# A last sum put behind the reads of its place, last branch rows loaded into their tiles, first pair parts split later

## The chip, the cores and the metric

The kernel runs on one core of a Trainium2 chip. The metric is the device time of one execution in microseconds (us), the median over several runs. TensorE (PE) does the matrix products; VectorE (DVE), ScalarE (ACT) and GpSimd (POOL) prepare and evacuate them; SyncE (SP) issues most of the DMAs.

## The reference

One layer of a hybrid encoder works on two streams of D = 1024 features: 1024 tokens of a new stream and 64 of a running one, 1088 columns in all. Cut to what matters:

```python
xn   = rmsnorm(x);  proj = xn @ w_in      # z | xBC | dt | q | k | v | gates
y    = rmsnorm((ssd(conv(xBC), dt) + d * xs) * silu(z))
o    = rmsnorm(diff_attention(rope(rmsnorm(q)), rope(rmsnorm(k)), v))
mix  = sigmoid(g_ssm) * (y @ w_branch_ssm) + sigmoid(g_att) * (o @ w_branch_attn)
x    = x + mix @ w_out
ha, hb = split(rmsnorm(x) @ w_up)
x    = x + (silu(conv(ha)) * hb) @ w_down
dt   = softplus(dt_raw + bias)            # the chain of small steps on VectorE
```

All is float32. The results are the two streams, and the new keys, values, states and convolution tails.

## The kernel before

**Three products for one.** TensorE multiplies rounded operands (type fp32r), so each float32 operand is split in two: a *cast* on ScalarE makes the high part (hi), and a *subtraction* on VectorE makes the rest (lo = source - hi). A product is the three matmuls hi·hi, hi·lo and lo·hi for each 128 rows of the contraction. The function split (L413 the cast, L414 the subtraction) does this, in place where the source was loaded into the lo tile. The function weights (L154 to L156) does the same for a whole weight block.

**Pairs.** The input projection (in_pair, L644), the up projection (L1604) and the down projection (L1778) work on two row blocks and the two column halves at once and need seven products in place of eight, numbered p = 0 to 6. Each has a left operand (a quarter of the weight block or a sum of quarters) and a right operand: the parts b11, t2, b21, t3, t1, t4, b22, which are quarters of the activations or sums of them. Every product has two column halves s = 0, 1, each 12 matmuls of 128x272. The left sums are made on GpSimd by make_left: s1 = q21 + q22 (L557), s2 = s1 - q11 (L559), s3 = q11 - q21 in q21's place (L561), and the last one, q12 - s2, in q12's place (L575). q12 itself is the left of p = 2, so its place is first read by that split. lefts_at is the table that says at which step of a pair each left is loaded, summed and split.

**Pair stage's start.** The first two pairs run their products p = 0 and 2 together (the list both), while the right parts t3, t1 and t4 are loaded from p_sc into their lo tiles and split by split_part. The table LATER says behind which p of the first pair the remaining parts are split. steps() is the dt chain: about 15 small VectorE instructions of 128x288 (L700 to L717), taken one by one beside the next pair.

**Branches.** branch() runs three times: the attention branch, and the two halves of the ssm branch. For each turn of output rows m in TURNS (the first turn is m = 0 and 1 together) it goes over four column chunks of 272 and makes a product of 8 row tiles x 3 matmuls (L162 to L164). The first two branches load both halves of their operand, split already, straight into the tiles, four row tiles per DMA (L206). The last branch has y_sc in float32 and stages it: a row tile of 128x272 is loaded into one of a few buffers b_f (L211), cast (L212) and subtracted (L213), 32 times. The tiles b{half}{chunk} are those of the branch before, so each is written only when TensorE has read it for the last time. Beside each product of the last branch lie loads into side tiles b_g (L192), a tanh (L220), a sum and product (L230 to L233) and the split of the mixed result (L1441, L1442).

The order on each engine is that of a scheduler that takes the instructions in program order with priorities and the waits that the tiles' reuse needs; an engine works its own queue in that order, and a wait at its head holds all behind it.

Of the kernel before, what the change touches and what calls it, by code (L numbers as in the profile page):

```python
# [90 lines left out]
def hybrid_layer(ctx: ExitStack, tc: tile.TileContext, xT, xt, prm, cst, rope, wvd, win, wbs, wba, wout, wup, wdn,  # L91
# [91 lines left out]
    def k_rows(parts, c, s):  # L183
        return [[t[:, k % 4] for t in parts[f"b{k // 4 + 1}{c + 1}", s]] for k in range(KT)]

    def branch(stage, side, src, wts, gates, adds, out, step=1):

        def next_to(m, c, w):
            tiles = []
# [10 lines left out]
        for i, (c, w) in enumerate(CH):  # L200
            tiles = {(f"b{h + 1}{i // 2 + 1}", i % 2): units_of(f"b{h + 1}{i // 2 + 1}", i % 2) for h in range(2)}
            parts.append(k_rows(tiles, i // 2, i % 2))
            for k in range(0, KT, step):
                if stage is None:
                    for u, t in enumerate(tiles[f"b{k // 4 + 1}{i // 2 + 1}", i % 2]):
                        load(out=t.bitcast(F32),  # L206
                             in_=src[D * u + P * k : D * u + P * (k + step), c : c + w].rearrange("(k p) t -> p k t", p=P))
                else:
                    t = stage()[:, :w]
                    hi, lo = parts[-1][k]  # L210
                    load(out=t, in_=src[P * k : P * (k + 1), c : c + w])  # L211
                    S.copy(hi, t)  # L212
                    V.tensor_tensor(out=lo, in0=t, in1=hi, op=ALU.subtract)  # L213
        for ms in TURNS:
            wt = [weights(wts[m], KT, P) for m in ms]
            for (c, w), rows_of in zip(CH, parts):
# [23 lines left out]
    def run(gen):  # L240
        for _ in gen:
            pass
# [294 lines left out]
    def make_left(x, what, blocks):  # L537

        if what == "load":
            for step in ("q11", "q21", "q22", "q12", "s1", "s2", "s3"):  # L540
                make_left(x, step, blocks)
            return
        if what in quarter:
            i, j = int(what[1]) - 1, int(what[2]) - 1
            n = blocks[i].shape[1] // 2
            seen["left"] = load(out=quarter[what][:, :n], in_=blocks[i][:, n * j : n * (j + 1)])
            return
        if what in ("s1", "s2", "s3"):
# [6 lines left out]
            q11, s2, q12, q21, s1, q22, q12 = made[x]  # L555
            if what == "s1":
                G.tensor_tensor(out=s1, in0=q21, in1=q22, op=ALU.add)  # L557
# [336 lines left out]
    rest = [(p, s) for p in (1, 3, 4, 5, 6) for s in range(2)]  # L894
    pairs = [begun_in(0), begun_in(1)]
    left[1] = {0: [t[:, :512] for t in early[1]], 2: [t[:, 512:] for t in early[1]]}
    for i, x in enumerate(("t3", "t1")):
        for at in both:
            pairs[i].send(at)
        split_part(x, seen["copy"])  # L900
        with after("copy"):
            for _ in range((2, 1)[i]):
                more_left(0)
    quarter_places()
    for at, (p, s) in enumerate(rest):
        pairs[0].send((p, s))
# [330 lines left out]
    with (tc.tile_pool(name="sin", bufs=1) as sin, tc.tile_pool(name="sp", bufs=1) as sp,  # L1237
# [163 lines left out]
                    load(out=d, in_=t)  # L1401
            yield i

        def stage():
            return staged("b_f")

        def side():
            return bs.tile([P, 384], F32, name="b_g", tag="b_g", bufs=BG)

        def branch_tiles():  # L1410
            nonlocal bs
            cv_pool.release()
            bs = tc.alloc_tile_pool(name="bs", bufs=1, side="right")
            yield from branch(None, side, o_sc, wba, D, (), store(m_sc), 4)
            yield from branch(None, side, y_sc[: 2 * D], wbs[0], None, (), store(n_sc), 4)

        bs, late = None, chain(filler, branch_tiles())
        for i in scan():
# [543 lines left out]
```

## Time and profile before

| | |
|---|---|
| median of 3 runs | 2444.05 us (2440.38 to 2444.22) |
| the profiled execution | 2447.51 us, of it a span of 2445.7 us |
| granted TensorE clock, mean | 0.995 |
| busy: PE, DVE, ACT, POOL | 98%, 71%, 50%, 28% |
| DMA, mean over the span | 184 GB/s |

TensorE is busy nearly always. What the other engines do moves the time only where TensorE stands waiting, or where its granted clock is lowered. The wait view lists each such place, and the windows view counts the matmuls that started in a stretch: where nothing is waited for, 5 us hold 42 matmuls of the 272-column kind in its counting, those on an edge included.

### The profile page before, as it was taken

The page shows a single profiled execution, that of the slowest core. Times are in us where ns is not written, and L with a number is a line of the kernel's source. Part 1 is how long each engine was busy: PE and PEld are TensorE (multiplying, and loading weights), DVE is VectorE, ACT ScalarE, POOL GpSimd, SP SyncE. Part 2 cuts the span into 40 slices and gives each one's busy share as a digit, 9 for nine tenths or more (in the row PEclk, how much of TensorE's full clock was granted, in tenths as well). Part 3 has the DMA queues.
Part 4 walks back from the last instruction along what each step waited for, and adds up shares of the span by engine and source line. Part 5 has one row for each costly group of instructions (what it writes and reads, how often), then busy time and mean ns, then how long its engine had stood idle before and what let it go on. Part 6 is the DMA issues. An engine that isn't in the chain of part 4 may idle for free.

```text
span 2445.7 us, 49558 instructions
## 1 busy us (share of the span) xinstructions
PE 2394.6 (98%) x18744; PEld 2320.2 (95%) x18744; DVE 1729.0 (71%) x3114; ACT 1227.7 (50%) x2713; POOL 686.3 (28%) x757
## 2 busy tenths in 40 slices
PE   8999999999999999999999999999999999999998
PEld 8989989999999999998899999999999999999998
DVE  4687877758687786867678665656966756768865
ACT  7345464356565665657555553434533333353442
POOL 0032333201011010115333332003255554544344
PEclk9999999999999999999999999999999999999999
DMA  7855768664544444336797954765124424357975
GB/s 245 275 175 188 240 206 298 207 204 148 163 150 149 129 146 143 108 123 227 260 330 249 336 182 131 225 198 172 56 84 144 158 97 157 128 191 198 253 181 104
DMA packets 296625, 449.80 MB, mean 184 GB/s; under 512 B 37113, under 2 KB 192898, under 8 KB 296386
## 3 DMA queue, kind: packets, MB, share of 16 engines
q1 hardware_dynamic: 285346, 420.31, 52.2%
q0 software_dynamic: 11040, 26.34, 5.3%
q8 instruction: 147, 2.41, 0.4%
q14 instruction: 92, 0.75, 0.1%
HBM read 294.03 MB, written 152.50 MB: 183 GB/s over the span
## 4 chain that ended last, share of the span: by engine, by line
PE 47%; DVE 3%; DMA 3%; issue 1%; POOL 1%; ACT 1%; SPq 0%; POOLq 0%; DVEq 0%; ACTq 0%
PE mx L1604 13%; PE mx L1778 6%; PE mm L1604 5%; PE mm L162 3%; PE mm L164 3%; PE mm L163 3%; PE mx L164 3%; PE mx L162 3%; PE mx L163 3%; PE mm L1778 2%; PE ye L1296 1%; PE yi L1290 1%; PE stp L1302 1%; DMA b_f<-y_sc 1%; DMA bc<-a_sc 1%
## 5 line engine op out<-in xcount | busy, mean ns | idle before, releaser
L162 PE MATMUL mm<-b,w_hi 128*128 128x272 f32 x1576 | 465.9, 296 | 0.3
L164 PE MATMUL mm<-b,w_lo 128*128 128x272 f32 x1576 | 459.2, 292 | 0.0
L163 PE MATMUL mm<-b,w_hi 128*128 128x272 f32 x1576 | 457.5, 291 | 0.0
L162 PEld LDWEIGHTS mm<-b,w_hi 128*128 128x128 f32 x1576 | 296.8, 188 | 6.2 <-issue 4.4
L163 PEld LDWEIGHTS mm<-b,w_hi 128*128 128x128 f32 x1576 | 297.0, 189 | 2.9 <-issue 2.1
L164 PEld LDWEIGHTS mm<-b,w_lo 128*128 128x128 f32 x1576 | 296.5, 188 | 0.7 <-issue 0.2
L985 DVE SCALAR_TENSOR_TENSOR cc<-pre,par,cc 128x272 f32<-128x272 f32 (+1 forms) x288 | 140.2, 490 | 16.3 <-ACT cc L983 13.4
L1604 PE MATMUL mx<-m,w_hi 128*128 128x272 f32 x752 | 144.4, 289 | 1.6 <-ACT m L413 1.3
L1604 PE MATMUL mx<-n,wh 128*128 128x272 f32 x1080 | 143.8, 288 | 1.9 <-DVE u L1631 1.0
L162 PE MATMUL mx<-b,w_hi 128*128 128x272 f32 x472 | 138.4, 295 | 3.2 <-ACT b L212 1.7
L1604 PEld LDWEIGHTS mx<-n,wh 128*128 128x128 f32 x1080 | 138.3, 188 | 2.5 <-DVE u L1631 1.3
L156 DVE TENSOR_TENSOR w_lo<-w_f,w_hi 128x1024 fp32r<-128x1024 f32 (+1 forms) x82 | 102.7, 1254 | 53.7 <-ACT w_hi L155 47.4
L414 DVE TENSOR_TENSOR wh<-w_f,wh 128x512 fp32r<-128x512 f32 (+1 forms) x144 | 140.4, 975 | 0.0
L973 POOL COPY pre<-pre 128x3 f32<-128x3 f32 x72 | 22.7, 315 | 419.0 <-DVE cc L987 195.9
L1109 ACT ACTIVATE p_t<-sc,mx 128x512 f32<-128x512 f32 (+6 forms) x144 | 106.1, 739 | 64.9 <-DVE mx L1100 30.9
L557 POOL TENSOR_TENSOR ws<-w_f 128x512 f32<-128x512 f32 (+1 forms) x47 | 62.4, 1328 | 270.4 <-DVE u L683 134.4
L164 PE MATMUL mx<-b,w_lo 128*128 128x272 f32 x472 | 137.5, 292 | 0.3 <-DVE w_lo L156 0.3
L163 PE MATMUL mx<-b,w_hi 128*128 128x272 f32 x472 | 136.2, 289 | 0.4 <-DVE b L213 0.3
L155 ACT CAST w_hi<-w_f 128x1024 fp32r<-128x1024 f32 (+1 forms) x82 | 85.9, 1049 | 71.8 <-PE mm L163 49.0
L1604 PEld LDWEIGHTS mx<-m,w_hi 128*128 128x128 f32 x752 | 118.0, 188 | 2.0 <-ACT m L413 1.5
L1613 ACT ACTIVATE cc<-pre,par 128x544 f32<-128x544 f32 (+1 forms) x44 | 37.2, 846 | 146.8 <-DVE pre L1648 145.8
L1604 PE MATMUL mx<-m,w_lo 128*128 128x272 f32 x376 | 108.3, 288 | 0.0
(463 smaller groups left out, 7101.4 us busy)
## 6 DMA issues: line engine op xcount, KB each, us to landing
w_f<-in_win_dram SPq DMA_DIRECT2D x48, 512.0 KB, 4.0
w_f<-in_wup_dram SPq DMA_DIRECT2D x80, 256.0 KB, 2.6
bc<-a_sc SPq DMA_DIRECT2D x32, 512.0 KB, 5.5
w_f<-in_win_dram SPq DMA_DIRECT2D x60, 256.0 KB, 3.9
h_sc<-hb SPq DMA_DIRECT2D x44, 272.0 KB, 2.1
ht<-h_sc SPq DMA_DIRECT2D x22, 544.0 KB, 4.8
t_sc<-ht SPq DMA_DIRECT2D x22, 544.0 KB, 2.9
out_dram<-yq POOLq DMA_DIRECT2D x44, 272.0 KB, 6.0
```

The costliest lines, as they stand in the source:

```text
L155: S.copy(hi, w)
L156: V.tensor_tensor(out=lo, in0=w, in1=hi, op=ALU.subtract)
L162: PE.matmul(ps, a_hi, b_hi, start=i == 0, stop=False)
L163: PE.matmul(ps, a_hi, b_lo, start=False, stop=False)
L164: PE.matmul(ps, a_lo, b_hi, start=False, stop=i == n - 1)
L414: V.tensor_tensor(out=lo, in0=src, in1=hi, op=ALU.subtract)
L557: G.tensor_tensor(out=s1, in0=q21, in1=q22, op=ALU.add)
L985: V.scalar_tensor_tensor(cc[:, :m], pre[:, i : i + m], cw(i), cc[:, :m], ALU.mult, ALU.add)
L1109: act(p_t[:n, :nk], sc[c][:n, :nk], AF.Exp, bias=mx[:n, c : c + 1], accum_out=dst)
L1604: PE.matmul(ps, w[x][:, c], b[y][:, k], start=start and k == i == 0, stop=k == 3 and i == 2, skip_group_check=not start)
L1613: act(cc[:, :n], pre[h][:, :n], AF.Identity, bias=col(O_FB + f), scale=cw(0))
L1778: PE.matmul(ps, w[y][:, c], b[z][:, k], start=start and k == j == 0, stop=k == n - 1 and j == 2, skip_group_check=not start)
```

## The change

Three edits:

- The sum q12 - s2 becomes a step of its own, "s4", in make_left. It was issued at the split of p = 3; now lefts_at issues it at step 1 of its pair, behind the split of p = 5. In the pairs that token_major names (the last one of the up projection, and in the down projection the first and last of each four) it is issued at step 0, and the split of p = 6 moves from step 0 to step 2.
- The last branch loads y_sc straight into the lo tiles, four row tiles per DMA (8 loads of 128x4x272), and splits them there with split (8 casts and 8 subtractions of 128x1088). The buffers b_f are gone from it.
- In the pair stage's start the split of t3 comes behind the products p = 0 and 2 of both first pairs, and those of t1, t4 and b22 behind p = 1, 3 and 4 of the first pair's rest; before, t3 came between the two pairs, t1 behind them, t4 behind p = 1 and b22 behind p = 3.

```diff
@@ branch()
-    def branch(stage, side, src, wts, gates, adds, out, step=1):
+    def branch(halves, side, src, wts, gates, adds, out):
...
-            for k in range(0, KT, step):
-                if stage is None:
+            for k in (0, 4):
+                if halves:
                     for u, t in enumerate(tiles[f"b{k // 4 + 1}{i // 2 + 1}", i % 2]):
                         load(out=t.bitcast(F32),
...
                 else:
-                    t = stage()[:, :w]
-                    hi, lo = parts[-1][k]
-                    load(out=t, in_=src[P * k : P * (k + 1), c : c + w])
-                    S.copy(hi, t)
-                    V.tensor_tensor(out=lo, in0=t, in1=hi, op=ALU.subtract)
+                    hi, lo = tiles[f"b{k // 4 + 1}{i // 2 + 1}", i % 2]
+                    load(out=lo.bitcast(F32), in_=src[P * k : P * (k + 4), c : c + w].rearrange("(k p) t -> p k t", p=P))
+                    split(hi, lo, lo.bitcast(F32))
@@ make_left()
+            elif what == "s4":
+                G.tensor_tensor(out=q12, in0=q12, in1=s2, op=ALU.subtract)
...
-        if what == 3:
-            G.tensor_tensor(out=made[x][6], in0=made[x][6], in1=made[x][1], op=ALU.subtract)
@@ lefts_at()
-            todo += {0: [(x, 6)]}.get(at, []) if token_major(x) else {0: [(x, 4)], 1: [(x, 5)], 3: [(x, 6)]}.get(at, [])
+            todo += ({0: [(x, "s4")], 2: [(x, 6)]} if token_major(x) else {0: [(x, 4)], 1: [(x, 5), (x, "s4")], 3: [(x, 6)]}).get(at, [])
@@ input projection
-    LATER = {1: "t4", 3: "b22"}
+    LATER = {1: "t1", 3: "t4", 4: "b22"}
...
-    for i, x in enumerate(("t3", "t1")):
+    for i in range(2):
         for at in both:
             pairs[i].send(at)
-        split_part(x, seen["copy"])
         with after("copy"):
             for _ in range((2, 1)[i]):
                 more_left(0)
+    split_part("t3", seen["copy"])
@@ run
-    run(branch(stage, side, y_sc[2 * D :], wbs[1], 0, (n_sc, m_sc), mixed))
+    run(branch(False, side, y_sc[2 * D :], wbs[1], 0, (n_sc, m_sc), mixed))
```

Lines behind L200 are numbered 2 to 5 lower in the changed kernel.

The order on ScalarE at the start of the pair stage, before. t300 to t311 are the tiles of t3 (hi of column half 0, its lo; hi of half 1, its lo), t100 to t111 those of t1, t400 to t411 of t4; w_hi are left operands, u1, pre and ss are what the first two pairs evacuate.

```order
L413 CAST t300_1580<-t301_1581 128x1088
L413 CAST t310_1583<-t311_1584 128x1088
L413 CAST w_hi_1676<-ws1_1602 128x512
L413 CAST w_hi_1676<-w_f_1600 128x512
L667 ACTIVATE ss_1762<-pre_1657 128x544
L700 ACTIVATE st_1567<-dtt_96 128x288
L715 ACTIVATE st_1567<-par_81 128x32
L679 COPY u1_1615<-mx_1696 128x272
L689 COPY pre_1722<-mx_1682 128x272
L701 ACTIVATE st_1567<-st_1567 128x288
L689 COPY pre_1722<-mx_1696 128x272
L413 CAST t100_1586<-t101_1587 128x1088
```

And in the changed kernel:

```order
L665 ACTIVATE ss_1758<-pre_1657 128x544
L698 ACTIVATE st_1567<-dtt_96 128x288
L713 ACTIVATE st_1567<-par_81 128x32
L677 COPY u1_1615<-mx_1692 128x272
L699 ACTIVATE st_1567<-st_1567 128x288
L687 COPY pre_1718<-mx_1678 128x272
L687 COPY pre_1718<-mx_1692 128x272
L411 CAST w_hi_1734<-ws2_1603 128x512
L411 CAST t300_1580<-t301_1581 128x1088
L411 CAST t310_1583<-t311_1584 128x1088
L411 CAST t100_1586<-t101_1587 128x1088
L411 CAST t110_1589<-t111_1590 128x1088
```

The casts of t3 stood ahead of the left operand's; now they stand behind them, behind the first ScalarE steps of the dt chain and behind the two copies L687 of the second pair's p = 2, and the casts of t1 follow at once.

The order on VectorE at the same place, before. st, dt2 and dtt are the tiles of the dt chain, w_lo the left operand's lo.

```order
L414 TENSOR_TENSOR t301_1581<-t301_1581,t300_1580 128x1088
L414 TENSOR_TENSOR t311_1584<-t311_1584,t310_1583 128x1088
L414 TENSOR_TENSOR w_lo_1677<-ws1_1602,w_hi_1676 128x512
L414 TENSOR_TENSOR w_lo_1677<-w_f_1600,w_hi_1676 128x512
L681 TENSOR_TENSOR u2_1614<-mx_1748,u1_1613 128x272
L712 TENSOR_SCALAR dtt_96<-dtt_96 128x288
L702 TENSOR_SCALAR st_1567<-st_1567 128x288
L681 TENSOR_TENSOR u2_1614<-mm_1784,u1_1613 128x272
L703 RECIPROCAL st_1567<-st_1567 128x288
L704 TENSOR_TENSOR st_1567<-st_1567 128x288
L683 TENSOR_TENSOR u1_1613<-mx_1748,u1_1613 128x272
L414 TENSOR_TENSOR t101_1587<-t101_1587,t100_1586 128x1088
```

And in the changed kernel, from the reciprocal on:

```order
L702 TENSOR_TENSOR st_1567<-st_1567 128x288
L703 TENSOR_TENSOR dt2_1951<-st_1567 128x288
L705 TENSOR_SCALAR st_1567<-dt2_1951 128x288
L679 TENSOR_TENSOR u2_1614<-mm_1780,u1_1613 128x272
L707 SCALAR_TENSOR_TENSOR st_1567<-st_1567,dt2_1951 128x288
L412 TENSOR_TENSOR w_lo_1735<-ws2_1603,w_hi_1734 128x512
L707 SCALAR_TENSOR_TENSOR st_1567<-st_1567,dt2_1951 128x288
L412 TENSOR_TENSOR t301_1581<-t301_1581,t300_1580 128x1088
L707 SCALAR_TENSOR_TENSOR st_1567<-st_1567,dt2_1951 128x288
L412 TENSOR_TENSOR t311_1584<-t311_1584,t310_1583 128x1088
L707 SCALAR_TENSOR_TENSOR st_1567<-st_1567,dt2_1951 128x288
L412 TENSOR_TENSOR t101_1587<-t101_1587,t100_1586 128x1088
```

The first of t3's subtractions stood ahead of the left operand's and of the whole dt chain; now a large part of the dt chain (L702 to L707) stands ahead of it, and steps of L707 between it and the next ones.

The order on ScalarE where the last branch begins, before. w_hi_19453 and w_hi_19459 are the weights of its first turn, b_g copies evacuate the branch before.

```order
L212 CAST b2100_19310<-b_f_19340 128x272
L212 CAST b1110_19344<-b_f_19348 128x272
L155 CAST w_hi_19453<-w_f_19452 128x1024
L226 COPY b_g_19177<-mx_19178 128x272
L226 COPY b_g_19205<-mm_19206 128x272
L226 COPY b_g_19233<-mm_19234 128x272
L212 CAST b1110_19344<-b_f_19352 128x272
L212 CAST b1110_19344<-b_f_19356 128x272
```

And in the changed kernel, where these weights are called w_hi_19349 and w_hi_19355:

```order
L411 CAST b1100_19308<-b1101_19309 128x1088
L411 CAST b2100_19310<-b2101_19311 128x1088
L224 COPY b_g_19121<-mx_19122 128x272
L224 COPY b_g_19149<-mx_19150 128x272
L411 CAST b1110_19318<-b1111_19319 128x1088
L155 CAST w_hi_19349<-w_f_19348 128x1024
L224 COPY b_g_19177<-mx_19178 128x272
L224 COPY b_g_19205<-mm_19206 128x272
L224 COPY b_g_19233<-mm_19234 128x272
L411 CAST b2110_19320<-b2111_19321 128x1088
L411 CAST b1200_19328<-b1201_19329 128x1088
L155 CAST w_hi_19355<-w_f_19354 128x1024
```

The eight row tiles of chunk 0 and the first one of chunk 1 stood ahead of the first weights, each alone; now tiles of four row tiles are cast whole, and the cast of chunk 1's first tile (b1110) stands ahead of the first weights.

The order on SyncE's queue there, in the changed kernel, where before 29 of the 32 loads into b_f stood among the stores and side loads up to the end of the first turn. n_sc and y_sc are stores of the branch before and of the scan.

```order
L210 DMA b1101_19309<-y_sc_74 128x4x272
L210 DMA b2101_19311<-y_sc_74 128x4x272
L236 DMA n_sc_71<-b_g_19093 128x272
L1335 DMA y_sc_74<-y_18762 128x4x320
L210 DMA b1111_19319<-y_sc_74 128x4x272
L236 DMA n_sc_71<-b_g_19121 128x272
L210 DMA b2111_19321<-y_sc_74 128x4x272
L236 DMA n_sc_71<-b_g_19149 128x272
L210 DMA b1201_19329<-y_sc_74 128x4x272
L210 DMA b2201_19331<-y_sc_74 128x4x272
L236 DMA n_sc_71<-b_g_19177 128x272
L236 DMA n_sc_71<-b_g_19205 128x272
```

Six of the eight loads stand in these rows, the last two a row further on.

More of the change, by code (lines that the diff above doesn't have):

```diff
@@ L202, in branch @@
             parts.append(k_rows(tiles, i // 2, i % 2))
[L203 to L204 removed]
+            for k in (0, 4):
+                if halves:
                     for u, t in enumerate(tiles[f"b{k // 4 + 1}{i // 2 + 1}", i % 2]):
                         load(out=t.bitcast(F32),
[L207 removed]
+                             in_=src[D * u + P * k : D * u + P * (k + 4), c : c + w].rearrange("(k p) t -> p k t", p=P))
                 else:
[L209 to L213 removed]
+                    hi, lo = tiles[f"b{k // 4 + 1}{i // 2 + 1}", i % 2]
+                    load(out=lo.bitcast(F32), in_=src[P * k : P * (k + 4), c : c + w].rearrange("(k p) t -> p k t", p=P))
+                    split(hi, lo, lo.bitcast(F32))
         for ms in TURNS:
@@ L547, in make_left @@
             return
-        if what in ("s1", "s2", "s3"):
+        if what in ("s1", "s2", "s3", "s4"):
             if what == "s1":
@@ L554, in make_left @@
                 left.setdefault(x, {})
-            q11, s2, q12, q21, s1, q22, q12 = made[x]
+            q11, s2, q12, q21, s1, q22, q12 = made[x][:7]
             if what == "s1":
                 G.tensor_tensor(out=s1, in0=q21, in1=q22, op=ALU.add)
+            elif what == "s4":
+                G.tensor_tensor(out=q12, in0=q12, in1=s2, op=ALU.subtract)
             elif what == "s2":
@@ L1402, in scan @@
             yield i
-        def stage():
-            return staged("b_f")
         def side():
@@ L1413, in branch_tiles @@
             bs = tc.alloc_tile_pool(name="bs", bufs=1, side="right")
-            yield from branch(None, side, o_sc, wba, D, (), store(m_sc), 4)
-            yield from branch(None, side, y_sc[: 2 * D], wbs[0], None, (), store(n_sc), 4)
+            yield from branch(True, side, o_sc, wba, D, (), store(m_sc))
+            yield from branch(True, side, y_sc[: 2 * D], wbs[0], None, (), store(n_sc))
         bs, late = None, chain(filler, branch_tiles())
```

## The prediction

> **What bounds the kernel now.** I read the busy times first, then the list of all waits of TensorE (PE), and then the windows and timelines at the places that the change touches.
>
> ```profile
> PE 2394.6 (98%) x18744; PEld 2320.2 (95%) x18744; DVE 1729.0 (71%) x3114; ACT 1227.7 (50%) x2713; POOL 686.3 (28%) x757
> ```
>
> TensorE is busy for 2394.6 of the 2445.7 us span, so work on the other engines costs nothing unless TensorE stands for it. Three places of the change are in its list of waits: the pair stage's start (115 to 170 us), the start of the last branch (1500 to 1570) and the down projection's first pairs (2170 to 2300). At the first:
>
> ```profile
> PE mx L644 <- DVE t L414: 3.0, 2, 2.0
> PE mx L644 <- ACT u L679: 1.0, 1, 1.0
> PE mm L644 <- DVE w_lo L414: 0.8, 1, 0.8
> ```
>
> ```profile
> 130.00:135.00 5.00, 4.91 (x40) 4.69 (x39) 4.97 (x10) 3.76 (x9) 0.14 (x1) 1.00 0.87 282
> 135.00:140.00 5.00, 2.63 (x19) 2.19 (x18) 5.00 (x4) 3.15 (x5) 4.77 (x4) 1.00 0.77 233
> 140.00:145.00 5.00, 4.00 (x19) 3.68 (x19) 5.00 (x6) 3.30 (x5) 3.48 (x2) 0.56 0.52 178
> 145.00:150.00 5.00, 5.00 (x33) 5.00 (x33) 5.00 (x8) 2.10 (x4) 0.00 (x0) 0.76 0.14 56
> 150.00:155.00 5.00, 5.00 (x42) 5.00 (x41) 5.00 (x12) 1.94 (x3) 0.00 (x0) 1.00 0.51 164
> 160.00:165.00 5.00, 4.22 (x34) 4.01 (x33) 4.87 (x6) 0.00 (x0) 4.08 (x3) 1.00 0.14 52
> ```
>
> The columns of a window are its length, then busy us and count for PE, PE's weight loads, DVE, ACT and POOL, the granted clock, and the DMA share. An undisturbed stretch (150 to 155) holds 42 matmuls. A missing matmul is 5 / 42 = 0.12 us lost, so the rows from 130 to 150 lose (2 + 23 + 23 + 9) x 0.12 = 6.8 us, and that from 160 another 1.0. The wait is for the parts that VectorE subtracts, and VectorE is busy for 5.00 of 5 us from 135 on: here it is the bound. Two of the stretches also have a lower clock, 0.56 and 0.76, behind the wait of 2.0 us.
>
> At the last branch:
>
> ```profile
> PE mx L162 <- ACT b L212: 1.7, 1, 1.7
> PE mx L162 <- ACT w_hi L155: 0.9, 1, 0.9
> ```
>
> ```profile
> 1515.00:1520.00 5.00, 5.00 (x42) 5.00 (x41) 1.39 (x4) 2.71 (x6) 0.00 (x0) 1.00 0.43 134
> 1535.00:1540.00 5.00, 4.74 (x36) 4.36 (x35) 4.05 (x11) 2.23 (x7) 0.00 (x0) 1.00 0.81 232
> 1540.00:1545.00 5.00, 4.81 (x32) 4.07 (x32) 4.02 (x10) 3.03 (x8) 0.00 (x0) 1.00 0.86 264
> 1545.00:1550.00 5.00, 2.88 (x19) 2.21 (x17) 2.23 (x7) 2.33 (x6) 0.00 (x0) 1.00 0.91 273
> 1550.00:1555.00 5.00, 3.95 (x29) 3.73 (x30) 3.66 (x9) 2.90 (x6) 0.00 (x0) 1.00 0.92 303
> ```
>
> Here the clock stays at 1.00 and (6 + 10 + 23 + 13) x 0.12 = 6.2 us are lost. Who is late is read from the two lines of the staged rows:
>
> ```profile
> L212 ACT CAST b<-b_f x32: 415/420/439, 1507.5 to 1547.8; 128x272 fp32r<-128x272 f32 x32
> ...
>   DMA b_f<-y_sc: 11.6, 19
> ```
>
> ```profile
> L211 SPq DMA_DIRECT2D b_f<-y_sc x32: 319/358/502, 1362.6 to 1544.3; - x32
> ...
> DMA to landing us min/median/max: 2.0/2.7/6.6
> ```
>
> ScalarE has only 13.4 us of casts, but stood 19 times, 11.6 us in all, for a row tile to land: three buffers, a landing of 2.7 us each and a queue of side loads between them make the staging slow. It runs to 1548, while the first turn began at 1520.9. And because the cast of the next weights stands behind the last row tile on ScalarE,
>
> ```profile
> 1549.68 1.04 ACT L155 CAST w_hi<-w_f 128x1024 fp32r<-128x1024 f32 x1
> ```
>
> they come at 1549.68 to 1550.7, which is the wait of 0.9 for w_hi.
>
> **The last branch's loads.** Removed are 32 loads, 32 casts and 32 subtractions; added are 8 loads of 544 KB, 8 casts and 8 subtractions of 128x1088. In engine time little changes: a cast of that size takes 1.05 us (two in 2.10, at 132.69 below) against 4 x 0.42 = 1.7. The gain is in when the rows arrive. The loads have places of their own, each free when TensorE has read it for the last time in the branch before. In the trace of before SyncE issues row tiles here from about 1507 on,
>
> ```profile
> 1508.46 1.07 SPq L211 DMA_DIRECT2D b_f<-y_sc  x2
> ```
>
> and chunk 0 of the new order goes there. TensorE frees a chunk's place about 6 us behind the one before (48 matmuls of 0.12), and between the loads stand stores, each held by the ScalarE copy that it stores; so I estimate chunk 1 at 1513 to 1515.5, chunk 2 by 1518 and chunk 3 by 1522. No such load is in the trace at this place. The nearest rows, by size and source, are those of the branch before:
>
> ```profile
> L206 SPq DMA_DIRECT2D b<-y_sc x16: 370/773/1927, 1358.1 to 1391.0; - x16
> ...
> DMA to landing us min/median/max: 4.8/8.9/10.2
> ```
>
> With those of the attention branch, which the line counts too, their median landing is 8.9, in a crowded stretch; the small ones at this very place take 2.7. The window at 1515 has a DMA share of only 0.43, so I take 4.5, between the two. Chunk 3 is then ready by 1529 with cast and subtraction, and is wanted at 1539; even at 10.2 it would be in time. The casts of the first turn end 20 us earlier, and the next weights are cast as soon as they land. So of the 6.2 us lost I let 0.7 remain, for chunk 0 to 1: **5.5 us gained**. The cover is the landing of chunk 1's first tile: its cast stands on ScalarE ahead of the first weights' (w_hi_19349). With 4.5 us it lands at 1517.7, the weights are cast by 1520 and subtracted by 1521.3 where TensorE wants them at 1520.9. At 8.9 they come at 1525.5 instead, which takes 4.5 of the gain back. Ends: 6.2 gained, and 4 lost (second rival).
>
> **The pair stage's start.** Nothing is removed; splits move. On ScalarE:
>
> ```profile
> 126.10 2.13 ACT L413 CAST t<-t 128x1088 fp32r<-128x1088 f32 x2
> 128.10 0.64 ACT L413 CAST w_hi<-ws 128x512 fp32r<-128x512 f32 x1
> ...
> 132.41 0.39 ACT L689 COPY pre<-mx 128x272 f32<-128x272 f32 x1 [1.24 <-PE mx L644]
> 132.69 2.10 ACT L413 CAST t<-t 128x1088 fp32r<-128x1088 f32 x2
> ```
>
> Before, the casts of t3 were done at 128.2, and TensorE had its high part ready when it came to it. Now they stand behind the copy at 132.41, which itself waits for TensorE's last product with the old parts; a left operand's cast (0.64) lies between. So t3's first high part is ready at about 132.4 + 0.3 + 0.6 + 1.05 = 134.3, with TensorE through all it had by 132.3. It stands for some 2 to 3 us there, where before it had work until 136. Whether this sets the end is decided by VectorE:
>
> ```profile
> 127.26 2.50 DVE L414 TENSOR_TENSOR t<-t,t 128x1088 fp32r<-128x1088 f32 x2 [5.86 <-ACT t L413]
> ...
> 134.71 1.28 DVE L414 TENSOR_TENSOR t<-t,t 128x1088 fp32r<-128x1088 f32 x1
> ...
> 137.38 2.36 DVE L414 TENSOR_TENSOR t<-t,t 128x1088 fp32r<-128x1088 f32 x1
> ...
> 140.82 2.37 DVE L414 TENSOR_TENSOR t<-t,t 128x1088 fp32r<-128x1088 f32 x1
> ...
> 143.47 2.01 DVE L414 TENSOR_TENSOR t<-t,t 128x1088 fp32r<-128x1088 f32 x1
> 145.41 0.71 DVE L671 TENSOR_TENSOR ss<-ss,sq 128x544 f32<-128x544 f32 x1
> 146.04 0.44 DVE L709 SCALAR_TENSOR_TENSOR st<-st,dt 128x288 f32<-128x288 f32 x1
> ```
>
> Before, it was busy without a gap from t3's subtraction at 127.26 to the end of t4's at 145.48, which includes much of the dt chain. In the new order it does the same up to that point, and more: five steps L709 (0.37 each by the next start) and the sum L671 (0.63), less one copy of pre (0.35): 5 x 0.37 + 0.63 - 0.35 = 2.1 us. It starts 0.5 earlier, since the left operand's casts now come first, and stands about as long for the chain's first ScalarE steps; these two I set against each other. What I keep is that four subtractions take 2.0 to 2.4 instead of 1.28 and so does the work beside GpSimd's sums:
>
> ```profile
> 134.86 2.28 POOL L557 TENSOR_TENSOR ws<-w_f 128x512 f32<-128x512 f32 x1 [134.41 <-DVE u L683]
> ```
>
> GpSimd's four sums still run, at about the same time, and the loss of VectorE beside them (1.08 + 1.09 + 0.73 = 2.9 us on three subtractions) only falls on t3 and t1 instead of t1 and t4. So t4 is through at 147.6, **2.1 us later**. After it TensorE has 11 matmuls left of t4. Before, these lay in the slow clock:
>
> ```profile
> 355.60 4.61 PE L644 MATMUL mx<-b,wh 128*128 128x272 f32 x21 [2.49 <-ACT u L679]
> ```
>
> is another such stretch, 21 matmuls in 4.61 us, 0.22 each, against 0.12. The stand of 2 to 3 us now comes some 5 us earlier, and so does the slow stretch; it then lies where VectorE is the bound anyway, and the last 11 go at 0.12: 11 x 0.10 = 1.1 us back. Behind that, the five steps L709 are done already, so the dt chain no longer delays the w_lo that TensorE waited 0.8 us for at 164.8; I count half. Sum: 2.1 - 1.1 - 0.4 = +0.6, and with some slow clock left I take **+1.0**. Ends: -3 if VectorE's work no longer falls beside GpSimd's, +5 if slow clock comes on top.
>
> [...]
>
> **The last sum s4.** On GpSimd its order against the other sums is the same nearly everywhere, since no other GpSimd work stood between its old place and its new one; the wait for the readers of q12 holds nobody else there. I cost it at 0 in the up projection, and the DMA share of its loads too. In the token-major pairs the split of p = 6 goes two steps back on ScalarE and VectorE, and u of the down projection goes ahead of the w_lo. TensorE's waits there are
>
> ```profile
> PE mx L1778 <- DVE n L414: 2.9, 2, 2.7
> PE mm L1778 <- DVE w_lo L414: 1.2, 1, 1.2
> ```
>
> The 1.2 us could go, or grow by the 0.4 of that copy; the 2.7 us at 2290 are a subtraction far down VectorE's queue that the move hardly touches. I take 0, within 2 either way. That two GpSimd output DMAs swap with sums there is cost at 0, since the sums are made some steps ahead of their split.
>
> **The sum.** 2447.5 (the profiled execution, 3.5 above the median) - 5.5 + 1.0 + 0 = 2443.0; the same 4.5 us off the median of 2444.05 is **2439.5 us**. A measurement of this kernel can tell about 0.2%, 4.9 us, from no change: 2439.2 to 2448.9 count as the same.
>
> **The rivals.**
> First, the splits save more than counted: TensorE's slow clock does not come in the pair stage, and VectorE's subtractions run in 1.28 beside an idle GpSimd. For it: GpSimd's first sum waits for loads that the earlier left splits release. Against: they are only some 3 us earlier. Pair stage -3, branch -5.5: 2444.05 - 8.5 = 2435.5.
>
> Second, slower: the last branch's loads land late. Chunk 1's first tile holds ScalarE's queue and with it the first weights. For it: the rows of the branch before, up to 10.2 us; four loads of 544 KB beside stores of n_sc. At 10.2 the tile lands at 1523.4, the weights are through (1.05 + 1.05 + 1.3) at 1526.8, 5.9 us after TensorE wants them, and a stand that long brings the slow clock of the windows at 140 and 145, (23 + 9) x 0.12 = 3.8 us: 9.7 against 5.5 gained, so +4.2, with +1.0 from the pair stage +5.2: 2449.3. It turns to a loss at a landing of about 7 us, where the wait of 2.7 and a slow stretch are more than the gain. Against: the DMA share of 0.43.
>
> Third, no gain: the first turn is paced by its side loads as soon as the rows are not. Each product of the last branch wants three of them, SyncE issues them behind one another, and they are not changed. Then half the 6.2 us stays, 2444.05 - 3.1 + 1.0 = 2442. The same band holds a pair stage with the slow clock on top, +3.8: 2444.05 - 5.5 + 1.0 + 3.8 = 2443.4. Against: TensorE's waits name the row tile and the weights, never a side load.
>
> **How the numbers follow.** Forecast 0.45, its own range 2437 to 2442, half of it under 2439.2; first rival 0.19; second 0.20; third 0.16. Faster: 0.225 + 0.19 = 0.42. Same: 0.225 + 0.16 = 0.38. Slower: 0.20. The range takes the ends of the first and second rival, since neither alone is under one in ten: 2434.5 to 2449.5.
>
> **What would show it.** Right: in the windows 1535 to 1555 the counts are 42 again, no wait for a part of the last branch is left, and the third turn's w_hi is cast by about 1542. Between 130 and 155 the count is about 8 matmuls lower in sum, with TensorE standing near 133 and t4's last subtraction ending near 147.6; the slow windows come at 135 to 145. Wrong: a wait for w_hi or w_lo at 1521 (late landing), waits for side tiles in the first turn, clock under 1.00 behind 145, or a difference at a place that is not named here.

## The result

The changed kernel's median is 2437.84 us (20 runs, 2432.04 to 2442.49), that of before 2443.57 (20 runs, 2439.64 to 2447.65). The ratio is 0.9979, with a 95% interval of 0.9972 to 0.9987: 5.1 us less, between 3.2 and 6.8. The difference of the medians is 5.7. The profiled execution took 2441.61 us, against 2447.51 before.

The head of the page after has the span and the busy times:

```profile
span 2439.8 us, 49478 instructions
...
PE 2393.0 (98%) x18744; PEld 2320.5 (95%) x18744; DVE 1719.7 (70%) x3090; ACT 1222.0 (50%) x2689; POOL 690.9 (28%) x757
```

TensorE has the same work; the span is 5.9 us shorter. The windows at the last branch's start, after:

```profile
1520.00:1525.00 5.00, 4.01 (x31) 3.77 (x31) 4.63 (x5) 4.88 (x9) 0.00 (x0) 1.00 1.10 351
...
1535.00:1540.00 5.00, 5.00 (x42) 5.00 (x41) 3.52 (x9) 1.29 (x4) 0.00 (x0) 1.00 0.59 165
1540.00:1545.00 5.00, 5.00 (x42) 5.00 (x41) 2.65 (x8) 2.43 (x7) 0.00 (x0) 1.00 0.84 237
1545.00:1550.00 5.00, 5.00 (x40) 4.78 (x39) 4.79 (x10) 2.86 (x5) 0.00 (x0) 1.00 0.54 177
1550.00:1555.00 5.00, 5.00 (x42) 5.00 (x41) 2.47 (x7) 1.17 (x3) 0.00 (x0) 1.00 0.83 285
```

The counts are 42 from 1525 on, but for 40 at 1545. Where 6.2 us were lost there are now (11 + 2) x 0.12 = 1.6. The wait view of that place, and the line of the new loads:

```profile
PE mx L164 <- DVE w_lo L156: 1.0, 1, 1.0
```

```profile
L210 SPq DMA_DIRECT2D b<-y_sc x8: 359/378/512, 1507.0 to 1522.7; - x8
...
DMA to landing us min/median/max: 3.7/5.1/5.7
```

The row tiles are no longer waited for. What is left is one wait for the first weights' low part. The loads land in 5.1 us in the median, and the last one was issued at 1522.7, where the last staged row went at 1544.3.

The pair stage's start, windows and waits after:

```profile
130.00:135.00 5.00, 2.94 (x22) 2.50 (x20) 4.93 (x10) 2.93 (x5) 0.00 (x0) 1.00 1.05 390
135.00:140.00 5.00, 3.39 (x15) 2.86 (x15) 5.00 (x4) 5.00 (x6) 3.93 (x3) 0.67 0.82 264
140.00:145.00 5.00, 4.34 (x22) 4.03 (x23) 5.00 (x4) 3.18 (x5) 2.49 (x2) 0.65 0.15 52
145.00:150.00 5.00, 4.57 (x36) 4.34 (x35) 5.00 (x10) 0.00 (x0) 0.00 (x0) 1.00 0.00 0
150.00:155.00 5.00, 5.00 (x42) 5.00 (x41) 5.00 (x10) 2.46 (x4) 0.57 (x1) 1.00 0.14 56
160.00:165.00 5.00, 5.00 (x41) 4.89 (x40) 3.35 (x7) 1.18 (x2) 4.14 (x3) 1.00 0.30 108
```

```profile
PE mx L642 <- DVE st L707: 1.5, 1, 1.5
PE mm L642 <- DVE t L412: 1.5, 2, 0.8
PE mx L642 <- DVE t L412: 1.2, 2, 0.8
```

TensorE stands near 133, before the part t3 is split, and the lower clock (0.67 and 0.65) has moved forward, from the stretch of 140 to 150 to that of 135 to 145. The windows from 160 on are nearly full, where before 8 matmuls were missing. And the waits of the down projection's first pairs:

```profile
PE mx L1773 <- DVE n L412: 1.4, 1, 1.4
PE mm L1773 <- DVE u L1787: 0.9, 1, 0.9
PE mx L1773 <- DVE m L412: 0.7, 1, 0.7
PE mx L1773 <- DVE u L1778: 0.4, 1, 0.4
```

These are 3.4 us in four waits, where the two lines of before that the prediction shows were 4.1 us in three. That for n, at 2290 before, fell from 2.7 to 1.4. The clock behind it is the third number from the end of the windows. Before:

```profile
2290.00:2295.00 5.00, 4.51 (x23) 4.51 (x24) 5.00 (x8) 1.68 (x4) 0.97 (x2) 0.66 1.11 292
```

After:

```profile
2285.00:2290.00 5.00, 4.38 (x31) 3.99 (x32) 5.00 (x8) 2.52 (x4) 0.95 (x2) 1.00 1.11 292
```

The stretch of 0.66 has gone from this place, and 8 matmuls more stand in the 5 us. But the changed kernel has a lower clock behind the other three waits, near 2210, where before it had none:

```profile
2210.00:2215.00 5.00, 4.16 (x29) 3.51 (x27) 5.00 (x7) 3.80 (x7) 3.96 (x2) 1.00 0.08 30
```

After:

```profile
2210.00:2215.00 5.00, 3.87 (x18) 3.65 (x19) 5.00 (x9) 0.62 (x1) 0.19 (x1) 0.70 0.59 111
```

So in this profile the slow stretch has moved and not gone; what the down projection gains lies in the waits.

### The profile page after: what moved, and what is told of

Its sections match the earlier page's. It is cut to its first block, busy times and chain, and to the rows that moved or that the text cites. A ratio compares the mean times of both kernels' runs of the same rounds, so it can differ in the third digit from the quotient of the medians.

```text
span 2439.8 us, 49478 instructions
## 1 busy us (share of the span) xinstructions
PE 2393.0 (98%) x18744; PEld 2320.5 (95%) x18744; DVE 1719.7 (70%) x3090; ACT 1222.0 (50%) x2689; POOL 690.9 (28%) x757
## 4 chain that ended last, share of the span: by engine, by line
PE 47%; DVE 4%; DMA 2%; issue 2%; ACT 1%; POOL 0%; SPq 0%; POOLq 0%; DVEq 0%; ACTq 0%
PE mx L1599 13%; PE mx L1773 6%; PE mm L1599 5%; PE mm L162 3%; PE mm L164 3%; PE mm L163 3%; PE mx L162 3%; PE mx L164 3%; PE mx L163 3%; PE mm L1773 2%; PE yi L1288 1%; PE ye L1294 1%; PE stp L1300 1%; PE tr L1267 1%; DMA w_f<-in_wout_dram 1%
## 5 line engine op out<-in xcount | busy, mean ns | idle before, releaser
L1616 POOL TENSOR_TENSOR hb<-hb,cc 128x544 f32<-128x544 f32 (+2 forms) x63 | 67.0, 1078 | 132.6 <-DVE hb L1637 98.5
```

The source lines that it names most:

```text
L1616: (V if f + 1 == FT else G).tensor_tensor(out=hb[h][:, o : o + n], in0=hb[h][:, o : o + n], in1=cc[:, d : d + n], op=ALU.mult)
```

## The experiments

A single profile is moved by a few us of the attention and the scan, so beside the times each run is read by stage, from the starts of the same matmuls in each trace. The pair stage runs from TensorE's wait for u (L679) near 126 to that near 356; the last branch from its wait for grs near 1505, such as

```profile
1505.72 0.39 PE L162 MATMUL mx<-b,w_hi 128*128 128x272 f32 x1 [0.52 <-ACT grs L1327]
```

to the up projection's first wait, near 1732; the down projection from its first matmul on the part n (L1778) to the end of the span. A bar is where the trace has no such wait at the start. The last two columns are the median and the ratio to the kernel before, measured beside it.

| kernel | pair stage | last branch | down projection | median us | ratio, 95% |
|---|---|---|---|---|---|
| before | 229.9 | 231.5 | 250.7 | | |
| changed | 230.4 | 226.9 | 249.4 | 2437.84 | 0.9979 (0.9972 to 0.9987) |
| branch alone | - | 226.8 | 250.6 | 2437.57 | 0.9967 (0.9955 to 0.9980) |
| pair stage alone | 229.6 | 231.7 | 251.8 | 2445.23 | 1.0007 (0.9997 to 1.0016) |
| s4 alone | 230.0 | 231.9 | 248.2 | 2442.00 | 0.9988 (0.9979 to 0.9997) |
| in place, one row tile each | 230.5 | 227.9 | 249.8 | 2437.76 | 0.9968 (0.9956 to 0.9980) |
| staged, eight buffers | 230.0 | 228.0 | 250.9 | 2440.67 | 0.9973 (0.9963 to 0.9983) |
| changed, pair stage as before | 230.0 | 229.0 | 250.5 | 2439.07 | 0.9966 (0.9955 to 0.9977) |
| that, and weights first | - | 229.6 | 248.4 | 2439.88 | 0.9975 (0.9964 to 0.9986) |
| changed, t3 early | 228.8 | 228.2 | 248.4 | 2438.41 | 0.9974 (0.9965 to 0.9983) |

The medians of before beside them were 2444.91 (the four of the first group: branch, pair stage, s4, one row tile each) and 2446.07 (the other four).

Kernels that have the same order of instructions in a stage show how far one profile of it can be trusted. The last branch took 226.8 to 229.0 us in the four that load four row tiles at a time with the weights where they were, and 231.5 to 231.9 in the three that stage in three buffers. The down projection took 248.2 to 250.5 in the six with the new left splits, and 250.6 to 251.8 in the four with the old. The pair stage can be read more sharply up to the 283rd matmul behind its start, near 170: 44.2 to 44.5 us in the six kernels with the old splits, 44.9 in the three with the new ones (changed, pair stage alone, one row tile each), and 42.8 with t3 early.

**The three parts alone.** The branch's loading alone, in the kernel before:

```diff
-                    t = stage()[:, :w]
-                    hi, lo = parts[-1][k]
-                    load(out=t, in_=src[P * k : P * (k + 1), c : c + w])
...
+                    hi, lo = tiles[f"b{k // 4 + 1}{i // 2 + 1}", i % 2]
+                    load(out=lo.bitcast(F32), in_=src[P * k : P * (k + 4), c : c + w].rearrange("(k p) t -> p k t", p=P))
+                    split(hi, lo, lo.bitcast(F32))
```

> The kernel before with the last branch's loading alone changed (8 loads of four row tiles in place). Theory: nearly all of the gain is here. The time is 4.5 us under before (ratio 0.998), no wait for a row tile is left in the first turn, one wait of about 1 us for w_lo at 1522 stays, and what follows the branch stands 4.5 us earlier in the profile. Rival (the first turn is paced by its side loads, and the gain comes from the pairs): half of it at most, 0 to -2 us, with waits for side tiles in the first turn.

The ratio is 0.9967, 8.1 us less (4.9 to 11.0), and the last branch is 4.7 us shorter. TensorE's wait there is the one foretold:

```profile
PE mx L164 <- DVE w_lo L156: 1.0, 1, 1.0
```

The rival falls: no wait for a side tile. The time is lower than the stage accounts for: the interval ends at 4.9, just above it. In this profile the attention and the scan were 4.7 us shorter as well, which the last section takes up.

The pair stage's splits alone:

```diff
-    LATER = {1: "t4", 3: "b22"}
+    LATER = {1: "t1", 3: "t4", 4: "b22"}
...
+    split_part("t3", seen["copy"])
```

> The kernel before with the later splits of the pair stage's start alone. Theory: VectorE is the bound there and gets more to do ahead of t4's last subtraction, so that ends near 149 in place of 145.5; the slow clock moves to 135 to 145, where it is covered; the first matmul behind the stage stands 0.5 us later (within 1), the time is the same within 1.5 us. Rival (the split costs a stand of TensorE and a slow clock on top): +3 to +5 us. Second rival (the move is what gained): -2 us or more.

The ratio is 1.0007 (0.9997 to 1.0016), the stage 0.3 us shorter. Its windows:

```profile
130.00:135.00 5.00, 2.37 (x15) 1.73 (x13) 4.93 (x10) 3.88 (x6) 0.00 (x0) 1.00 1.05 386
135.00:140.00 5.00, 3.75 (x17) 3.42 (x18) 5.00 (x4) 4.91 (x7) 4.88 (x3) 0.60 0.67 214
140.00:145.00 5.00, 4.34 (x28) 4.02 (x27) 5.00 (x6) 2.42 (x4) 1.55 (x2) 0.72 0.15 52
```

The stand is at 130 to 135 (15 matmuls of 42) and the slow clock at 135 to 145, as in the changed kernel. Neither of the two rivals is borne out; a cost of up to 3.9 us is within the interval of the time. The length of the whole stage does not show one; up to the 283rd matmul the stage is 0.6 us longer than before.

The last sum's move alone:

```diff
+            elif what == "s4":
+                G.tensor_tensor(out=q12, in0=q12, in1=s2, op=ALU.subtract)
...
-        if what == 3:
-            G.tensor_tensor(out=made[x][6], in0=made[x][6], in1=made[x][1], op=ALU.subtract)
...
-            todo += {0: [(x, 6)]}.get(at, []) if token_major(x) else {0: [(x, 4)], 1: [(x, 5)], 3: [(x, 6)]}.get(at, [])
+            todo += ({0: [(x, "s4")], 2: [(x, 6)]} if token_major(x) else {0: [(x, 4)], 1: [(x, 5), (x, "s4")], 3: [(x, 6)]}).get(at, [])
```

> The kernel before with the last sum moved alone. Theory: the order on GpSimd hardly changes, so the time is the same within 1 us up to the down projection, and within 2 us at the end. Rival (the move relieves the token-major pairs): the waits at 2200 to 2220 and at 2290 fall by 2 us or more and the time by as much.

Here the rival came true. The ratio is 0.9988 (0.9979 to 0.9997), 2.9 us less, and the down projection is 2.5 us shorter. The wait for n fell from 2.7 to 0.7:

```profile
PE mx L1778 <- DVE n L414: 0.7, 1, 0.7
```

VectorE reached that subtraction earlier, and in part because it had waited less. ScalarE's casts of the parts ph, which come back from t_sc, show it. In the kernel before (the bracket is ScalarE's idle time, and what ended it):

```profile
2273.09 1.10 ACT L413 CAST ph<-ph 128x1088 fp32r<-128x1088 f32 x1 [2.48 <-DMA ph<-t_sc]
...
2277.04 1.10 ACT L413 CAST ph<-ph 128x1088 fp32r<-128x1088 f32 x1 [1.41 <-DMA ph<-t_sc]
```

With s4 and the split of p = 6 moved:

```profile
2266.37 1.10 ACT L413 CAST ph<-ph 128x1088 fp32r<-128x1088 f32 x1 [0.40 <-DMA ph<-t_sc]
...
2270.91 1.11 ACT L413 CAST ph<-ph 128x1088 fp32r<-128x1088 f32 x1
```

ScalarE stood 3.9 us for the two loads before, and 0.4 now; VectorE, whose subtractions of ph follow, had 1.4 us of waits for them and has none. In the four kernels with the old left splits (before, branch alone, pair stage alone, eight buffers) and the six with the new ones this divides without exception: 2.8 to 4.5 us in sum with the old, 0 to 0.6 with the new. So does the wait for n, 2.65 to 2.70 against 0.4 to 2.1.

The second of these ranges is wide, and the six kernels have the same order of instructions on every engine there. What tells them apart is the first of the subtractions of n. In the kernel before VectorE takes 2.38 us for it, beside GpSimd's third left sum (L561, from 2281.43 to 2283.18):

```profile
2281.95 2.38 DVE L414 TENSOR_TENSOR n<-n,n 128x1088 fp32r<-128x1088 f32 x1
```

With s4 alone it takes 1.28:

```profile
2276.21 1.28 DVE L414 TENSOR_TENSOR n<-n,n 128x1088 fp32r<-128x1088 f32 x1
```

Three of the six have 1.28 (s4 alone, weights first, t3 early), with a wait for n of 0.4 to 0.7 and a down projection of 248.2 to 248.4. The other three have 2.38 (changed, one row tile each, changed with the pair stage as before), with waits of 1.4 to 2.1 and 249.4 to 250.5. So the loads of ph are a part of the fall, and much of the rest goes with the time of that subtraction, 1.28 or 2.38 us, which differs between profiles of the same order.

Why the load of ph stands 2 us earlier is seen only in the order: on SyncE two loads of weights stand behind loads and stores of right parts that they stood ahead of, and on VectorE the sums that fill t_sc stand some rows further forward. Which of these does it was not tried. When the split of p = 6 is moved by itself, and the sum is left where it was, the order of the instructions is the same on every engine as with both. So the sum's own move does nothing that the order shows, and the gain is that of the later split of p = 6.

**What made the staging slow.** In place, with one row tile per load:

```diff
-                    load(out=lo.bitcast(F32), in_=src[P * k : P * (k + 4), c : c + w].rearrange("(k p) t -> p k t", p=P))
-                    split(hi, lo, lo.bitcast(F32))
+                    for r in range(4):
+                        load(out=lo[:, r].bitcast(F32), in_=src[P * (k + r) : P * (k + r + 1), c : c + w])
+                        split(hi[:, r], lo[:, r], lo[:, r].bitcast(F32))
```

> The changed kernel, with the last branch's rows loaded into place one row tile at a time: 32 loads of 128x272, 32 casts and 32 subtractions as before, but no staging buffers. If the place makes the gain (no load waits for a buffer to be emptied by VectorE), the time is within 1 us of the changed kernel and the first turn has no waits for rows. If the size of the loads makes it (few large transfers, few queue entries on SyncE and ScalarE), 3 us or more are lost again, with waits for row tiles in the first turn as before.

0.9968: the same as the large loads. In the first turn TensorE waits for no row tile. It waits for the first weights' low part (0.4), and once for the next weights:

```profile
PE mx L162 <- ACT w_hi L155: 1.7, 1, 1.7
...
PE mx L164 <- DVE w_lo L156: 0.4, 1, 0.4
```

And staged as before, but with eight buffers:

```diff
         def stage():
-            return staged("b_f")
+            staged_at[0] += 1
+            if staged_at[0] % 8 < 3:
+                return staged("b_f")
+            return bs.tile([P, 272], F32, name="b_f", tag="b_f", bufs=5)
...
-            return bs.tile([P, 384], F32, name="b_g", tag="b_g", bufs=BG)
+            return bs.tile([P, 272], F32, name="b_g", tag="b_g", bufs=BG)
```

> The kernel before, with staged row tiles in the last branch as they were, but eight buffers b_f instead of three (room for them comes from side tiles cut to the 272 columns that are used). Theory: what made the staging slow is that a load waits for a buffer to be read by ScalarE and VectorE. With eight the loads run ahead of the first turn, its waits for row tiles go, and 3 to 5 us are gained, nearly as much as by loading in place. Rival (32 small loads, casts and subtractions in queues with stores and side loads are slow by themselves): under 2 us gained, and waits for row tiles stay in the first turn.

0.9973, 6.6 us less, and the last branch 3.5 us shorter. The casts of the staged rows:

```profile
L212 ACT CAST b<-b_f x32: 412/420/440, 1505.3 to 1527.2; 128x272 fp32r<-128x272 f32 x32
...
  DMA b_f<-y_sc: 3.4, 4
```

They ended at 1527 instead of 1548, and ScalarE stood 3.4 us for rows in place of 11.6. So neither the size of the loads nor the number of casts made the staging slow, but the three buffers. How they did it stands in the order of SyncE's queue. With eight buffers every load is issued ahead of the first side load, the last at 1524.2 and the side load at 1524.6. With three, 17 of them stand among the side loads, from 1524.7 to 1544.3. Ahead of the loads SyncE waited 9.1 us from 1510 on with three buffers, 8.2 of it for VectorE, and 4.0 with eight. So a load could go only when its buffer had been read, and few buffers also put it far back in the queue.

**The rest.** The changed kernel with the pair stage as before:

```diff
-    LATER = {1: "t1", 3: "t4", 4: "b22"}
+    LATER = {1: "t4", 3: "b22"}
...
-    split_part("t3", seen["copy"])
```

> The changed kernel with the pair stage's splits where they were before. Theory: the later splits cost 0 to 1 us, so this is 0 to 1 us faster than the changed kernel and about 7 us (ratio 0.997) under before: 4.7 from the last branch, 2 from the down projection. Rival (the later splits gain): slower than the changed kernel by 2 us or more.

0.9966 (0.9955 to 0.9977), and the pair stage is 230.0 us long, 0.4 shorter than with the later splits. The interval of the time overlaps that of the changed kernel, so the time does not tell the cost apart from nothing; up to the 283rd matmul the stage is 0.6 us shorter. That the later splits gained is not borne out.

With the first weights ahead of chunk 1's first tile:

```diff
+        first = None
+        if not halves:
+            first, behind = [], []
+            for m in TURNS[0]:
+                first.append(weights(wts[m], KT, P))
+                behind += [seen["w_hi"], seen["w_lo"]]
...
+                    with ExitStack() as pins:
+                        if i == 1:
+                            for x in behind[:2]:
+                                pins.enter_context(tc.issue_after(x.ins))
+                        split(hi, lo, lo.bitcast(F32))
```

> As the one without the later splits, and the first turn's first weights are cast and subtracted ahead of chunk 1's first tile in the last branch. Theory: the wait of 1.0 us for w_lo at the first turn's start comes from that tile's cast and subtraction standing ahead on ScalarE and VectorE; it goes, and the first turn starts 1 us earlier. In the time that is within noise: ratio 0.996 to 0.997. Rival (the weights wait for TensorE to give up their buffer, not for the queue): the wait stays.

0.9975, and the last branch is no shorter. The wait of 1.0 for w_lo at the start has gone, but two of about 0.5 took its place (the other half of the first line lies in the next turn):

```profile
PE mx L164 <- ACT w_hi L157: 1.0, 2, 0.6
...
PE mm L164 <- ACT b L423: 0.5, 1, 0.5
```

These are for the second weights and for a tile of the rows (mm b). The rival is out, since the wait went. The theory had the cause of the wait, and missed that ScalarE has little time to spare there whatever stands first: it was busy for 4.88 of the 5 us from 1520 in the changed kernel's window above.

The changed kernel with t3's split early:

```diff
-    for i in range(2):
+    for i, x in enumerate(("t3", None)):
         for at in both:
             pairs[i].send(at)
+        if x:
+            split_part(x, seen["copy"])
...
-    split_part("t3", seen["copy"])
```

> The changed kernel with t3's split alone put back between the two first pairs; t1, t4 and b22 stay later. Theory: TensorE's stand at 132 to 135 and the slow clock at 135 to 145 come from t3's split; with it early, TensorE works through there, the stand comes at 136 to 140 as before, and the stage ends within 1 us of the changed kernel's, because VectorE has the same work up to t4's last subtraction. Rival (t3's move is what costs): the stage ends 1.5 us or more earlier than in the changed kernel.

The pair stage is 228.8 us, 1.5 less than the changed kernel's and 1.1 less than before's: the rival, by one profile. Up to the 283rd matmul it took 42.8, against 44.9 with all splits later and 44.2 to 44.5 with all of them early. So, by this one profile, t3's later split costs about 2.0 us there, and the later splits of the others give back about 1.5. The windows:

```profile
130.00:135.00 5.00, 4.91 (x39) 4.69 (x38) 5.00 (x10) 3.78 (x9) 0.00 (x0) 1.00 0.91 285
135.00:140.00 5.00, 2.60 (x18) 2.11 (x16) 5.00 (x5) 4.71 (x6) 4.61 (x3) 1.00 0.77 247
140.00:145.00 5.00, 4.83 (x26) 4.83 (x26) 5.00 (x4) 1.96 (x4) 3.83 (x4) 0.66 0.42 157
145.00:150.00 5.00, 4.15 (x29) 3.57 (x29) 5.00 (x9) 1.69 (x3) 0.00 (x0) 1.00 0.14 56
```

TensorE works through 130 to 135 (39 of 42); the stand is at 135 to 140 as before, with one slow stretch in place of two. The time, 0.9974, cannot tell this from the changed kernel. No version is shown to beat the changed one.

## Why the prediction was right

The forecast was 2439.5 in a range of 2434.5 to 2449.5, and 4.5 us less than before; 2437.84 and 5.7 less were measured. By its terms:

**The last branch, -5.5.** This term was over. It is -4.6 by the windows of the changed kernel and -4.7 with the branch alone, but those are the two shortest: the mean of the four with this order is 4.0 less than that of the three that stage in three buffers. The landing was put at 4.5 and is 5.1. Chunk 1's first tile was to land at 1517.7; its cast began at 1518.4, and the weights behind it were the wait of 1.0 that was named, a little more than the 0.7 left in the sum. The third turn's weights were to be cast by 1542; their cast began at 1544.7, and TensorE did not wait for it. The second rival, late landing, needed about 7 us; the slowest of these loads took 5.7. The sign that the prediction gave for it, a wait for w_lo at 1521, did come, but it was 1.0 us, with the clock at 1.00 behind it. The third, pacing by side loads, is refuted by the waits, which name no side load. That the buffers were the cause is shown by the two runs on the staging.

**The pair stage, +1.0.** Over the whole stage the kernels with the new splits of all parts (changed, alone, one row tile each) are at 229.6 to 230.5, those with the old at 229.9 to 230.0: +0.2. Up to the 283rd matmul, where they scatter less, it is +0.5, close to the +0.6 that was summed before the allowance. Two of its steps were off and cancelled. t4's last subtraction was to end 2.1 us later, at 147.6; it ended at 148.95, 3.5 later. Of this 0.55 is the later start of the stage in this profile: counted from there it ends at 22.7 in all three kernels, against 19.5 to 19.8 in the six with the old splits, 2.9 later:

```profile
134.87 1.29 DVE L412 TENSOR_TENSOR t<-t,t 128x1088 fp32r<-128x1088 f32 x1
136.07 1.54 DVE L707 SCALAR_TENSOR_TENSOR st<-st,dt 128x288 f32<-128x288 f32 x1
137.53 2.37 DVE L412 TENSOR_TENSOR t<-t,t 128x1088 fp32r<-128x1088 f32 x1
139.82 1.53 DVE L707 SCALAR_TENSOR_TENSOR st<-st,dt 128x288 f32<-128x288 f32 x1
141.28 3.57 DVE L412 TENSOR_TENSOR t<-t,t 128x1088 fp32r<-128x1088 f32 x2
...
146.47 2.48 DVE L412 TENSOR_TENSOR t<-t,t 128x1088 fp32r<-128x1088 f32 x2
```

Two of the five steps L707 of the dt chain ran beside GpSimd's sums (136.00 to 137.30 and 138.72 to 141.04) and took 1.5 us instead of 0.45, which had not been counted; another step, 1.55 before (L705 there), took 0.46. Against that, the slow stretch lies earlier and is covered: with one row tile each the clock is 0.77 and 0.89 there in place of 0.67 and 0.65, and the stage is no shorter. And the wait of 0.8 for w_lo at 165 has gone altogether, where half had been counted. The matmuls between 130 and 155 were to be 8 fewer and are 16 fewer, 137 against 153, four or five of them by the later start. The first rival is not borne out: the slow clock did come, and subtractions of 2.4 us are still there.

No stand of TensorE is longer than 1.5 us here, and matmuls lie between them; still the clock is 0.50 from 136.67 to 143.49, which makes the 0.67 and 0.65. In the 5 us ahead of it TensorE stood for 2.9 us in sum.

**The last sum, 0.** This term was mis-sized: -2.5 in its own profile, and -1.9 as the mean of the six kernels with it (248.2 to 250.5) against the four without (250.6 to 251.8); the measured time fell by 2.9. The step that failed is "the 2.7 us at 2290 are a subtraction far down VectorE's queue that the move hardly touches". The move did touch it, through the loads of ph that ScalarE and VectorE had waited for 15 us earlier, and in three profiles of six through a subtraction of n that took 1.28 us in place of 2.38. The bound of 2 us either way holds for the mean alone.

So -4.0, +0.5 and -1.9 make -5.4 where -4.5 had been summed, and 5.1 by the ratio was measured. The total came out right in part by luck: the first term was over by 1.5 and the last under by 1.9.

## What to carry to other kernels

Where a group of small loads feeds a chain of casts and each is waited for, count the buffers before the bytes: eight buffers did as well as loading in place. When splits are moved along a queue, follow the loads on which the instructions behind them stand, not only the wait that ends last on the bounding engine; here a wait of 2.7 us was in part made by loads 15 us earlier. And a place that stands for several reasons gives back less than the one that is removed, as the weights that were put first show. A gain of 1 or 2 us in a stage wants several profiles of the same order, or the length of a shorter stretch, before it is believed.

## What was not expected of the hardware

The waits alone do not tell where the lower clock comes. In the up projection's start TensorE has two waits, of 0.8 and 1.0 us before and of 0.9 and 1.0 in the changed kernel. Before, the clock stays at 1.00 behind them:

```profile
1735.00:1740.00 5.00, 3.15 (x23) 2.71 (x23) 5.00 (x11) 1.14 (x2) 0.00 (x0) 1.00 0.52 171
1740.00:1745.00 5.00, 4.97 (x39) 4.75 (x39) 5.00 (x8) 3.32 (x5) 0.00 (x0) 1.00 0.00 0
```

After, with the same order of instructions there, it falls:

```profile
1730.00:1735.00 5.00, 3.13 (x20) 2.69 (x20) 5.00 (x11) 1.14 (x2) 0.00 (x0) 0.91 0.45 172
1735.00:1740.00 5.00, 5.00 (x32) 5.00 (x32) 5.00 (x8) 2.52 (x4) 0.00 (x0) 0.75 0.00 0
```

TensorE stood for 1.85 of the 5 us from 1735 before, and for 1.87 of those from 1730 after. From that second wait to the next one 10.5 us pass before and 11.6 after; the kernels with s4 alone and with one row tile each have 10.5 and 11.6 as well. These two stood for 1.84 and 1.85 of the 5 us from 1730, and in the 5 us behind them the clock was 1.00 and 0.66.

From 100 us to 2425 us the clock is lower in five stretches of the profile of before, which begin at 140.6, 355.6, 461.4, 1171.4 and 2291.0, and in five of the changed kernel's, at 136.7, 460.9, 1170.9, 1734.1 and 2212.0. It is 0.50 in each, and a figure such as 0.66 is the mean of a view of 5 us: before, the clock was 0.50 from 2290.96 to 2294.37 and 1.00 in the rest of the 5 us from 2290. In the 5 us ahead of each of the ten TensorE stood for 1.9 to 3.1 us in sum. But in the changed kernel it also stood for 2.9 of the 5 us from 355, where before had its second stretch, and there the clock was 1.00 and stayed at it. So neither the longest wait nor the sum over 5 us tells where it comes, and what decides was not shown.

The stretch from TensorE's wait at 460, the last of the input projection, to the wait for grs took 1045.3 us in the profile of before and 1041.5 with s4 alone, and these two have the same order of instructions in it on every engine. Over the four kernels with staged rows it is 1041.5 to 1045.3, over the six that load in place 1040.3 to 1045.0. So a few us of any two single runs differ there without a cause in the kernel, and whether the new loads gain there too stays open. Kernels with the same order in a stage differ there by up to 1 us in the pair stage, 2.2 in the last branch and 2.3 in the down projection; the whole time of one run differs by 8, which is the spread of the 20 of before.
